# Projecting the last 512 tokens' values within attention instead of ahead of it

## The chip, the cores and the metric

The kernel runs on one core of a Trainium2 chip. The core has five engines that run their own instruction streams: TensorE (PE in the profile; its weight loads are shown apart as PEld), VectorE (DVE), ScalarE (ACT), GpSimd (POOL) and SyncE (SP, which here issues the DMAs). The metric is the device time of one execution in microseconds (us); lower is better. The kernel before takes 2252.64 us, the median of three runs (2252.49 to 2254.42).

## What is computed

One decoder block on 2048 tokens of 1024 channels. Cut to the part that matters here:

```python
h = rmsnorm(x, g_mix_pre) * (1.0 + scale_m) + shift_m
q, k, v, u = split(h @ w_in, [512, 1024, 1536])       # 512 channels each
attn = stick_breaking_attention(heads(q), heads(k), heads(v))   # 8 heads of 64 channels
pool = pooling_mixer(u, w_pool, pool_scale)
x = x + gate_m * rmsnorm(concat(attn, pool) @ w_out, g_mix_post)
# then a SwiGLU FFN of width 2816 in the same sandwich
```

Stick-breaking attention is causal: for each query, sigmoid(-z) of the earlier keys is multiplied up from the nearest key outwards, and a key's weight is sigmoid(z) times that product. Everything is float32. A float32 product is made of three TensorE matmuls on operands that are split in a high part (a cast to the `fp32r` type) and a low part (what is left): high x high, high x low, low x high.

## The kernel before

**Blocks.** The 2048 tokens are four blocks of 512 (`tb` 0 to 3). [...]

**Stages.** First the conditioning vectors and the q, k and u projections of blocks 0 and 1. Then the **v stage** (170 to 271 us in the profile): `v_pieces` projects the values of all 2048 tokens, block by block in the order 1, 0, 2, 3, each in four groups of 128 tokens (tokens as the stationary operand, all 512 value channels as the moving one; 8 pieces of 3 matmuls a group). Each group's result goes to `store_v`: ACT casts the high part into a tile `ve`, DVE subtracts for the low part, and SP stores it to `vd[tb]` in HBM. `weave` puts side work between the pieces: it is given generators with a first piece and a distance, and takes one step of a generator whenever the count of pieces has reached its next place. Among them are `token_ops(2)` and `token_ops(3)` (normalising and turning the tokens of blocks 2 and 3) and `out_weight_ops`, which loads w_out in 16 jobs of 128 x 512 floats, splits each in two (ACT the high part, POOL or DVE the low one, into `wo_parts`, which has four places), multiplies the first eight jobs by the pooling maps (three matmuls into a bank `wf`, then a split of that), and stores both parts in `wod`. One job loads 256 KB and stores 512 KB.

Then **attention** (from 271 us to about 790 us). Its work is a list of 320 steps (80 units of a head, a query block and a key block, four steps each). A step gives TensorE two score matmuls `z`, up to four transposes of a finished weight tile (`wt`, 128 x 128 each), and two value matmuls `av`. ACT takes two sigmoids of `z` and the cast of `wt`; DVE the running product (a scan along the keys) and the low part of `wt`; POOL the product of the two. In a diagonal unit (query block = key block) the four steps are 128, 256, 384 and 512 keys wide, in the others all are 512 wide: 32 diagonal units and 48 full ones.

**Filler.** Between the steps stand the projections of q, k and u for blocks 2 and 3, as **filler**: `pieces` makes them in tasks of 8 pieces of 3 matmuls (weights of 128 channels as the stationary operand, 512 tokens as the moving one), with one more empty piece per task. 12 chunks of 128 channels and two blocks make 24 tasks. The main loop takes as many pieces as the share of attention already done asks for (`goal`, spread over the first 79 of the 80 units), so a larger number of pieces is spread more densely over the same steps. The result of a task is taken out of its PSUM bank by `take_chunk`: a q or k chunk is split by ACT and DVE into a tile `e` of the pool `wst` (one buffer), and stored.

**Order.** For PE, ACT, DVE and POOL the order of instructions is the order of the program (`manual_schedule`). A step's place in the loop is thus its place in each engine's queue. The order of DMAs on SP is left to the scheduler. Memory of the v stage is used again by attention: the first `pr` tiles (the running products) lie where the last `ve` tiles lay, so they wait until those tiles' stores have landed.

In attention the transposes' results go to three PSUM banks in turn (`t_ps`: w0, w1, a1), the scores to two, and the filler to one (`mm`).

Of the kernel before, what the change touches and what calls it, by code (L numbers as in the profile page):

```python
# [9 lines left out]
F32 = mybir.dt.float32  # L10
# [34 lines left out]
def block_kernel(ctx, tc, x, c, w_cond, b_cond, g_mix_pre, g_mix_post, w_in, w_pool,  # L45
# [11 lines left out]
    def split(hi, lo, src, low=nc.vector):  # L57

        nc.scalar.copy(hi, src)  # L59
        low.tensor_tensor(lo, src, raw(hi), ALU.subtract)  # L60
# [285 lines left out]
    def token_ops(tb):  # L346

        new_tokens(tb)
        xs = normed_rows(tb, 0)
        yield  # L350
        for j in range(4):
            nxt = normed_rows(tb, j + 1) if j < 3 else None
            yield from put_tokens(tb, j, xs)
            xs = nxt
# [80 lines left out]
            else:  # L435
                op()

    base = {"q": 0, "k": SBW, "u": 3 * SBW}

    def chunk_load(chunk, th, pair=None, w32=None):  # L440
        kind, m = chunk
# [59 lines left out]
    def take_chunk(chunk, tb, ps):  # L501
        kind, m = chunk
        if kind == "u":
            ops = pool_ops(tb, ps, m)
            urgent.append(next(ops))
            small.append(ops)
        else:
            urgent.append(lambda: store_qk(tb, ps, (qd if kind == "q" else kd)[m], f"{kind}{m}"))

    def v_pieces(wvs, pool):  # L510
        for tb in (1, 0, 2, 3):
            for j in range(4):
                if (tb, j) == (1, 3):
                    turn[0] += 1
                ps = mm_ps(f"v{tb}_{j}")
                cols = slice(j * P, (j + 1) * P)
                for k in range(KC):
                    mm3(ps, [(tokens(tb, k, cols), (wvs[0][:, k, :], wvs[1][:, k, :]))],
                        first=k == 0, last=k == KC - 1)
                    if k == KC - 1:  # L520
                        urgent.append(lambda a=(tb, j, ps, pool): store_v(*a))
                    run_small()
                    yield
# [11 lines left out]
    def weave(main, sides):  # L535

        done = [0] * len(sides)
        for n, _ in enumerate(main):
            for i, (ops, first, every) in enumerate(sides):
                if n >= first + done[i] * every:  # L540
                    done[i] += 1
                    next(ops, None)
        for ops, _, _ in sides:
            for _ in ops:
                pass
# [265 lines left out]
    def pool_map_ops():  # L811

        pool = wvs[0]
        p32 = spare[:, 0].rearrange("p (k n) -> p k n", k=KC)
        nc.sync.dma_start(p32[:, 0:NG], w_pool.rearrange("g p n -> p g n"))
        yield
        for g in range(NG):
            wp.append([pool.tile([P, P], F32R, tag=f"wp{n}{g}", bufs=1, name=f"wp{n}{g}") for n in "hl"])
            pt = t_ps(f"wpt{g}")
            nc.tensor.transpose(pt[:, 0:P], p32[:, g], ident)  # L820
            nc.vector.tensor_scalar_mul(p32[:, g], pt[:, 0:P], colv[:, 64 + g:65 + g])
            yield
            split(*wp[g], p32[:, g])
            yield

    def out_weight_ops():

        w32 = hc.tile([P, KC, TB], F32, tag="hi", name="wo32")
        parts = hc.tile([P, 2, 4, TB], F32R, tag="lo", name="wo_parts")
        jobs = [(k, half) for k in (4, 5, 6, 7, 0, 1, 2, 3) for half in range(2)]  # L830

        def load(i):
            k, half = jobs[i]
            nc.sync.dma_start(w32[:, i % KC], w_out[k * P:(k + 1) * P, half * TB:(half + 1) * TB])

        def store(i):
            k, half = jobs[i]
            for l in range(2):
                nc.sync.dma_start(wod[k][l][:, half * TB:(half + 1) * TB], raw(parts[:, l, i % 4]))

        for i in range(4):
            load(i)
        for _ in range(6):
            yield
        pss = {}
        for i in range(len(jobs) + 1):
            if i < len(jobs):
                split(parts[:, 0, i % 4], parts[:, 1, i % 4], w32[:, i % KC], (nc.gpsimd, nc.vector)[i % 2])
                if jobs[i][0] < 4:
                    store(i)  # L850
            if i + 4 < len(jobs):
                load(i + 4)
            yield
            if i in pss:
                split(parts[:, 0, (i - 2) % 4], parts[:, 1, (i - 2) % 4], pss[i])
                store(i - 2)
                yield
            if i and jobs[i - 1][0] >= 4:
                pss[i + 1] = av_ps(f"wf{i}")
                mm3(pss[i + 1], [(wp[jobs[i - 1][0] - 4], (parts[:, 0, (i - 1) % 4], parts[:, 1, (i - 1) % 4]))])  # L860
                yield
# [4 lines left out]
    def first_filler_ops():  # L866
        for part in range(4):
            chunk_split(first_filler, part)
            yield
# [17 lines left out]
    def first_unit_loads():  # L887
        qts[0, 0] = wst.tile([P, 2, TB], F32R, tag="e", bufs=1, name="qt0_0")
        load_queries(qts[0, 0], 0, 0)
        yield  # L890
        load_keys(up.tile([P, TB], F32R, tag="um", bufs=2, name="kt0_0"),
                  up.tile([P, 16 + TB], F32R, tag="us0", name="vt0_0")[:, 0:TB].rearrange("p (b e) -> p b e", e=P), 0, 0)
        yield

    weave(v_pieces(wvs[1:], wvs[0]), [(token_ops(2), 30, 3), (token_ops(3), 62, 3), (pool_map_ops(), 2, 2), (out_weight_ops(), 34, 2), (first_filler_ops(), 20, 4), (first_unit_loads(), 108, 6)])
    drain_small()
    pro.close()

# [6 lines left out]
    def block_loads(h, tb):  # L905
        qt = qkp.tile([P, 2, TB], F32R, tag="qt", name=f"qt{h}_{tb}")
        load_queries(qt, h, tb)
        for sc in {0: (0,), 1: (1,), 2: (2, 1, 0), 3: (3,)}[tb]:
            load_keys(qkp.tile([P, TB], F32R, tag="kt", bufs=6, name=f"kt{h}_{tb}_{sc}"),
                      att.tile([P, 4, P], F32R, tag="vt", bufs=6, name=f"vt{h}_{tb}_{sc}"), h, sc)  # L910
        return qt
# [73 lines left out]
    def unit_loads(u):  # L985
        h, tb, sc = u
        if sc == tb and (h, tb) not in qts:
            assert tb < 2 or {("q", h // 2, tb), ("k", h // 2, tb)} <= stored
            qts[h, tb] = block_loads(h, tb)

    chunks = []
    for hp in range(4):
        chunks += [("q", hp), ("k", hp)]
        chunks += [("u", g) for g in {1: (0,), 3: (1, 2, 3)}.get(hp, ())]

    def fillers():
# [1 line left out]
        while urgent:  # L998
            urgent.pop(0)()

    tasks = [(n, tb) for n in range(len(chunks) - 2) for tb in (2, 3)]
    tasks += [(n, tb) for tb in (2, 3) for n in (len(chunks) - 2, len(chunks) - 1)]
    fill = fillers()
    N_PIECES = 9 * 2 * len(chunks) + 1
    units = [(h, tb, sc) for half in range(2) for h in range(HEADS) for tb in (2 * half, 2 * half + 1) for sc in range(tb, -1, -1)]
    area = [2.5 if tb == sc else 4.0 for _, tb, sc in units]
    wo, wo_next = [], 0
# [859 lines left out]
```

## Time and profile before

The profile is of one execution, whose span is 2250.0 us; the median of the runs, 2252.64 us, is 2.64 us above that span, which is what lies around it and the difference from run to run.

| stage, us from the span's start | what TensorE does | PE busy | DVE busy | ACT busy | POOL busy |
|---|---|---|---|---|---|
| 170 to 272 | values, side work | 102.00 of 102 | 48.32 | 53.32 | 28.64 |
| 272 to 815 | attention with filler, first products with w_out | 538.44 of 543 | 514.66 | 473.73 | 427.45 |
| 1100 to 1150 | FFN products alone, a piece of the stage that runs to the end | 50.00 of 50 | 33.39 | 14.14 | 40.02 |

How to read it: "busy" sums the time of an engine's instructions. A matmul is shown longer than the distance to the next one, since they are pipelined and their ends are modelled (389 ns are shown for a 128x512 matmul, though the next one starts 227 ns later). DVE and ACT instructions overlap their followers too, by some 0.1 us. So whether an engine still has room is read from the distance between starts in the timeline, not from its busy share.

### The profile page before, as it was taken

The numbers are of one execution on the slowest core, as the hardware profiler recorded it, in microseconds if no ns is written. First come the engines' busy times: TensorE is split into PE (matmuls) and PEld (weight loads), VectorE is DVE, ScalarE is ACT, GpSimd is POOL, SyncE is SP. The second block draws the span as 40 slices with busy tenths as digits, with TensorE's granted clock in tenths as the row PEclk, the third lists the DMA queues.
The fourth block names the chain that finished last, engine by engine and source line by source line (L and its number), as shares of the span: only waits on it lengthen the run. The fifth ranks groups of instructions, "written<-read, shape, count | busy, mean of one in ns | idle before, by whom it ended". The sixth has DMA issues, their size and how long they took to land.

```text
span 2250.0 us, 33310 instructions
## 1 busy us (share of the span) xinstructions
PE 2227.7 (99%) x10613; PEld 1844.9 (82%) x10613; DVE 1612.7 (72%) x2227; ACT 1168.1 (52%) x2425; POOL 1270.2 (56%) x1579
## 2 busy tenths in 40 slices
PE   8999999999999999999999999999999999999998
PEld 6888888888888888888888888888888888888887
DVE  7874599999999956666565656787965565655566
ACT  6335599898999944453232323555532323234444
POOL 1452277787779955546868687221677565651003
PEclk9999999999999999999999999999999999999999
DMA  9996877534443556665555556777853333328664
GB/s 317 343 283 212 282 205 183 148 107 114 121 123 104 164 178 221 226 203 170 162 161 159 164 162 209 252 233 244 253 169 122 94 117 94 116 90 297 213 188 149
DMA packets 324205, 413.56 MB, mean 184 GB/s; under 512 B 20855, under 2 KB 189371, under 8 KB 323901
## 3 DMA queue, kind: packets, MB, share of 16 engines
q1 hardware_dynamic: 319420, 408.81, 57.4%
q10 hardware_dynamic: 4608, 2.63, 0.4%
q8 instruction: 83, 1.36, 0.3%
q14 instruction: 94, 0.76, 0.1%
HBM read 282.90 MB, written 128.45 MB: 183 GB/s over the span
## 4 chain that ended last, share of the span: by engine, by line
PE 86%; DVE 5%; POOL 3%; issue 2%; ACT 2%; DMA 1%; DVEq 0%; POOLq 0%; ACTq 0%
PE wt L961 4%; PE t_g L71 4%; PE t_u L70 4%; PE t_g L70 4%; PE t_u L71 4%; PE t_u L69 4%; PE t_g L69 4%; PE dn0p L69 3%; PE dn0p L71 3%; PE dn0p L70 3%; PE dn1p L69 3%; PE dn1p L70 3%; PE dn1p L71 3%; PE b_u L70 3%; PE b_g L70 3%; PE b_g L71 3%
## 5 line engine op out<-in xcount | busy, mean ns | idle before, releaser
L950 POOL TENSOR_TENSOR w<-sg,pr 128x512 f32<-128x512 f32 (+2 forms) x320 | 306.3, 957 | 46.4 <-DVE pr L945 13.8
L1350 POOL TENSOR_TENSOR s<-s,cu 128x512 f32<-128x512 f32 x88 | 133.4, 1521 | 236.9 <-DVE cu L1349 128.3
L945 DVE TENSOR_TENSOR_SCAN pr<-pr,carry,begin 128x512 f32<-128x512 f32 x192 | 244.3, 1273 | 0.0
L929 ACT ACTIVATE sg<-z 128x512 f32<-128x512 f32 (+2 forms) x320 | 183.1, 572 | 50.9 <-PE z L927 40.5
L60 DVE TENSOR_TENSOR wtl<-wt,wth 128x512 fp32r<-128x512 f32 (+1 forms) x320 | 190.2, 594 | 17.8 <-ACT wth L59 15.5
L59 ACT CAST wth<-wt 128x512 fp32r<-128x512 f32 (+1 forms) x320 | 181.8, 568 | 10.4 <-PE wt L961 8.0
L931 ACT ACTIVATE pr<-z 128x512 f32<-128x512 f32 (+2 forms) x320 | 182.2, 569 | 0.0
L961 PE MATMUL wt<-ident,w 128*128 128x128 f32 x1088 | 172.3, 273 | 1.5 <-POOL pr L941 1.1
L60 DVE TENSOR_TENSOR u_s_l<-u_s,u_s_h 128x512 fp32r<-128x512 f32 x66 | 64.1, 971 | 151.2 <-ACT u_s_h L59 151.1
L961 PEld LDWEIGHTS wt<-ident,w 128*128 128x128 f32 x1088 | 134.1, 140 | 32.7 <-POOL pr L941 1.8
L1340 ACT ACTIVATE s<-s 128x512 f32<-128x512 f32 x88 | 55.7, 632 | 180.5 <-DVE s L1339 180.5
L976 PE MATMUL av<-wth,vt 128*128 128x512 f32 (+1 forms) x320 | 126.1, 394 | 0.9 <-ACT o L981 0.8
L60 DVE TENSOR_TENSOR u_a_l<-u,u_a_h 128x512 fp32r<-128x512 f32 x66 | 72.9, 1105 | 65.6 <-ACT u_a_h L59 65.4
L69 PE MATMUL dn0p<-w0p_h,g0p_h 128*128 128x512 f32 x308 | 119.8, 389 | 0.0
L70 PE MATMUL dn0p<-w0p_l,g0p_h 128*128 128x512 f32 x308 | 119.8, 389 | 0.0
L71 PE MATMUL dn0p<-w0p_h,g0p_l 128*128 128x512 f32 x308 | 119.8, 389 | 0.0
L926 PE MATMUL z<-kt,qt 128*128 128x512 f32 (+2 forms) x320 | 118.6, 371 | 0.7 <-ACT pr L931 0.6
L977 PE MATMUL av<-wtl,vt 128*128 128x512 f32 (+1 forms) x320 | 117.8, 368 | 1.3 <-DVE wtl L60 1.2
L59 ACT CAST u_s_h<-u_s 128x512 fp32r<-128x512 f32 x66 | 38.6, 614 | 151.9 <-POOL u_s L1282 150.2
L927 PE MATMUL z<-kt,qt 128*128 128x512 f32 (+2 forms) x320 | 117.0, 365 | 0.0
L59 ACT CAST g_s_h<-g_s 128x512 fp32r<-128x512 f32 x66 | 39.5, 621 | 148.2 <-POOL g_s L1282 72.0
L69 PE MATMUL dn1p<-w1p_h,g1p_h 128*128 128x512 f32 x292 | 113.6, 389 | 0.0
(657 smaller groups left out, 7173.1 us busy)
## 6 DMA issues: line engine op xcount, KB each, us to landing
g<-in_w_gate_dram SPq DMA_DIRECT2D x42, 512.0 KB, 5.4
u<-in_w_up_dram SPq DMA_DIRECT2D x42, 512.0 KB, 4.4
wc<-in_w_cond_dram SPq DMA_DIRECT2D x32, 512.0 KB, 7.6
qt<-qd SPq DMA_DIRECT2D x64, 256.0 KB, 4.0
kt<-kd SPq DMA_DIRECT2D x96, 128.0 KB, 3.6
vt<-vd SPq DMA_DIRECT2D x48, 256.0 KB, 3.9
wd<-in_w_down_dram SPq DMA_DIRECT2D x44, 256.0 KB, 3.7
tdt<-wd SPq DMA_DIRECT2D x44, 256.0 KB, 2.0
```

Of the source, the lines that this page charges most:

```text
L59: nc.scalar.copy(hi, src)
L60: low.tensor_tensor(lo, src, raw(hi), ALU.subtract)
L69: nc.tensor.matmul(ps, lh, rh, start=first and i == 0, stop=False)
L70: nc.tensor.matmul(ps, lh, rl, start=False, stop=False)
L71: nc.tensor.matmul(ps, ll, rh, start=False, stop=last and i == n - 1)
L929: nc.scalar.activation(sg[:, 0:L], z[:, 0:L], AF.Sigmoid, scale=0.125)
L931: nc.scalar.activation(pr[:, 0:L], z[:, 0:L], AF.Sigmoid, scale=-0.125)
L945: nc.vector.tensor_tensor_scan(keys, keys, begin, carry, ALU.mult, ALU.bypass)
L950: nc.gpsimd.tensor_tensor(w[:, 0:L], sg[:, 0:L], pr[:, 1:L + 1], ALU.mult)
L961: nc.tensor.transpose(wt[:, i * P:(i + 1) * P], wss[u][i][:, b * P:(b + 1) * P], ident)
L976: nc.tensor.matmul(av[:, lo0:], vb, wh[:, lo0:], start=first, stop=False)
L1350: nc.gpsimd.tensor_tensor(s, s, u, ALU.mult)
```

## The change

```diff
-    base = {"q": 0, "k": SBW, "u": 3 * SBW}
+    base = {"q": 0, "k": SBW, "v": 2 * SBW, "u": 3 * SBW}
...
             small.append(ops)
+        elif kind == "v":
+            urgent.extend(turn_values(tb, ps, m))
         else:
             urgent.append(lambda: store_qk(tb, ps, (qd if kind == "q" else kd)[m], f"{kind}{m}"))
 
+    def turn_values(tb, ps, hp):
+
+        v32 = att.tile([P, TB], F32, tag="v32", bufs=1, name=f"v32_{hp}")
+
+        def turn():
+            pt = t_ps(f"vt{hp}")
+            for j in range(4):
+                nc.tensor.transpose(pt[:, j * P:(j + 1) * P], v32[:, j * P:(j + 1) * P], ident)
+            ve = wst.tile([P, HEADS, 2, DH], F32R, tag="e", bufs=1, name=f"ve{tb}_{hp}")
+            split(ve[:, :, 0, :], ve[:, :, 1, :], pt.rearrange("p (g d) -> p g d", d=DH))
+            nc.sync.dma_start(vd[tb].rearrange("(j p) h e -> p j h e", p=P)[:, :, 2 * hp:2 * hp + 2, :],
+                              raw(ve.rearrange("p (j h) l d -> p j h (l d)", h=2)))
+            stored.add(("v", hp, tb))
+
+        return [lambda: nc.scalar.copy(v32, ps), lambda: None, turn]
+
     def v_pieces(wvs, pool):
-        for tb in (1, 0, 2, 3):
+        for tb in (1, 0, 2):
...
-    weave(v_pieces(wvs[1:], wvs[0]), [(token_ops(2), 30, 3), (token_ops(3), 62, 3), (pool_map_ops(), 2, 2), (out_weight_ops(), 34, 2), (first_filler_ops(), 20, 4), (first_unit_loads(), 108, 6)])
+    weave(v_pieces(wvs[1:], wvs[0]), [(token_ops(2), 30, 3), (token_ops(3), 62, 3), (pool_map_ops(), 2, 2), (out_weight_ops(), 34, 1.5), (first_filler_ops(), 20, 4), (first_unit_loads(), 82, 6)])
...
             assert tb < 2 or {("q", h // 2, tb), ("k", h // 2, tb)} <= stored
+            assert tb < 3 or ("v", h // 2, tb) in stored
...
-        chunks += [("q", hp), ("k", hp)]
+        chunks += [("q", hp), ("k", hp), ("v", hp)]
...
-    tasks = [(n, tb) for n in range(len(chunks) - 2) for tb in (2, 3)]
+    tasks = [(n, tb) for n in range(len(chunks) - 2) for tb in (2, 3) if chunks[n][0] != "v" or tb == 3]
...
-    N_PIECES = 9 * 2 * len(chunks) + 1
+    N_PIECES = 9 * len(tasks) + 1
```

The values of block 3 leave the v stage: 96 of its 384 matmuls go, with four `store_v`. They come back as four tasks of filler in attention, one for each pair of heads, placed behind that pair's q and k: 96 matmuls again, now with the value weights stationary, so that the result has channels on the partitions and tokens along the row. It must be turned: ACT copies the bank to `v32`, TensorE makes four transposes into a bank of `t_ps`, ACT and DVE split that into `ve`, and SP stores it. The chunk's weights (512 KB a chunk) are loaded and split as other chunks' are, in four parts by ACT and POOL. There are 28 tasks in place of 24, 253 pieces in place of 217. In the v stage, which now has 96 pieces in place of 128, a step of `out_weight_ops` is taken every 1.5 pieces in place of 2, and the loads of the first unit are asked for from piece 82 in place of 108.

The instruction orders below are those of the two programs, without times. A name's numbers count its buffers; lines of the changed kernel are 18 further on behind the new function, and 19 behind the changed list of tasks.

On ACT, at the end of the v stage, before (`wo_parts` is a half of a job's split, `ve` the cast of a group of values, `sg` and `pr` the first sigmoids of attention):

```order
L59 CAST wo_parts_1910<-wf8_2453 128x512
L59 CAST wo_parts_1910<-wo32_1909 128x512 x3
L59 CAST ve3_0_2518<-v3_0_2475 128x8x64
L59 CAST wo_parts_1910<-wo32_1909 128x512 x3
L59 CAST ve3_1_2562<-v3_1_2522 128x8x64
L59 CAST ve3_2_2596<-v3_2_2566 128x8x64
L59 CAST ve3_3_2625<-v3_3_2600 128x8x64
L929 ACTIVATE sg0_0_0_0_2665<-z0_0_0_0_2662 128x128
L931 ACTIVATE pr0_0_0_0_2667<-z0_0_0_0_2662 128x128
```

and now:

```order
L59 CAST ve2_2_2461<-v2_2_2379 128x8x64
L59 CAST wo_parts_1910<-wo32_1909 128x512 x2
L337 CAST hth3_2166<-x3_3_h1_2451 128x4x128
L59 CAST wo_parts_1910<-wo32_1909 128x512
L59 CAST ve2_3_2509<-v2_3_2469 128x8x64
L947 ACTIVATE sg0_0_0_0_2549<-z0_0_0_0_2546 128x128
L949 ACTIVATE pr0_0_0_0_2551<-z0_0_0_0_2546 128x128
```

Three casts of values stood between the last split of w_out and attention's first sigmoid; now one does.

On SP, the DMAs at the same place, before (`wod` are the stores of w_out, `vd` those of values, `qt`, `kt` and `vt` the loads of attention's second unit):

```order
L839 DMA wod3_173<-wo_parts_1910 128x512 x4
L528 DMA vd3_95<-ve3_1_2562 128x1024
L528 DMA vd3_95<-ve3_2_2596 128x1024
L876 DMA qt0_1_2721<-qd0_1_61 64x2x512 x2
L882 DMA kt0_1_1_2724<-kd0_1_77 64x512
L528 DMA vd3_95<-ve3_3_2625 128x1024
L882 DMA kt0_1_1_2724<-kd0_1_77 64x512
```

and now:

```order
L546 DMA vd2_94<-ve2_2_2461 128x1024
L857 DMA wod2_172<-wo_parts_1910 128x512
L857 DMA wod3_173<-wo_parts_1910 128x512 x4
L546 DMA vd2_94<-ve2_3_2509 128x1024
L894 DMA qt0_1_2605<-qd0_1_61 64x2x512 x2
L900 DMA kt0_1_1_2608<-kd0_1_77 64x512 x2
L901 DMA vt0_1_1_2609<-vd1_93 128x4x128
```

Between the last stores of w_out and the loads of the second unit there is one store of values now, in place of three.

On PE, in attention, where the first turned values now stand (`q1_2` is the filler's next task, `vt0_4032` the bank of turned values, `av` attention's own products with the loaded values `vt4_0_0`); before, no such rows exist:

```order
L69 MATMUL q1_2_4005<-hth2_1858,wq1_1_h_3659 128x512
L70 MATMUL q1_2_4005<-htl2_1859,wq1_1_h_3659 128x512
L71 MATMUL q1_2_4005<-hth2_1858,wq1_1_l_3660 128x512
L519 MATMUL vt0_4032<-ident_180,v32_0_3932 128x128 x4
L994 MATMUL av4_0_4026<-wth4_0_0_1_3977,vt4_0_0_3749 128x384
L995 MATMUL av4_0_4026<-wtl4_0_0_1_3978,vt4_0_0_3749 128x384
```

The four transposes stand behind a piece of the next task, two pieces after the copy to `v32` was put in ACT's queue.

## The prediction

> **What bounds the kernel now.** First the page's busy times, then the windows by stage (columns: PE, PEld, DVE, ACT and POOL busy with their counts, granted clock, DMA share, GB/s), since an average over the span says nothing of one stage.
>
> ```profile
> PE 2227.7 (99%) x10613; PEld 1844.9 (82%) x10613; DVE 1612.7 (72%) x2227; ACT 1168.1 (52%) x2425; POOL 1270.2 (56%) x1579
> 206.00:244.00 38.00, 38.00 (x190) 31.40 (x189) 26.56 (x55) 28.82 (x63) 15.03 (x15) 1.00 0.71 243
> 244.00:266.00 22.00, 22.00 (x98) 18.21 (x98) 8.29 (x11) 8.42 (x16) 6.63 (x5) 1.00 0.96 359
> 273.50:412.20 138.70, 135.90 (x793) 114.78 (x792) 132.28 (x190) 125.29 (x312) 98.08 (x230) 1.00 0.74 197
> 412.20:788.70 376.50, 374.74 (x2102) 312.50 (x2101) 367.40 (x458) 339.84 (x752) 315.31 (x675) 1.00 0.44 124
> 1100.00:1150.00 50.00, 50.00 (x222) 41.44 (x221) 33.39 (x40) 14.14 (x26) 40.02 (x27) 1.00 0.51 162
> ```
>
> In the v stage PE has no gap, at a full clock. In attention (the rows that start at 273.50 and 412.20, together 515.2 us) PE and DVE are both near their whole time, so busy shares can't tell which one leads. The distances between starts can. PE in mid-attention, most of a full step and then a piece of filler (start, length, engine, line):
>
> ```profile
> 551.91 0.39 PE L977 MATMUL av<-wtl,vt 128*128 128x512 f32 x1
> 552.14 0.39 PE L926 MATMUL z<-kt,qt 128*128 128x512 f32 x1
> 552.38 0.39 PE L927 MATMUL z<-kt,qt 128*128 128x512 f32 x1
> 552.61 0.60 PE L961 MATMUL wt<-ident,w 128*128 128x128 f32 x4
> 552.96 0.48 PE L69 MATMUL k<-hth,wk_h 128*128 128x512 f32 x1
> 553.28 0.40 PE L70 MATMUL k<-htl,wk_h 128*128 128x512 f32 x1
> 553.51 0.40 PE L71 MATMUL k<-hth,wk_l 128*128 128x512 f32 x1
> 553.75 0.39 PE L976 MATMUL av<-wth,vt 128*128 128x512 f32 x1
> ```
>
> A 128x512 matmul starts 0.233 us after the one before (551.91 to 552.61, three of them); four transposes take 0.35, and the matmul after the next one comes 0.08 late, so 0.11 a transpose. There is no gap: with its filler PE is full. All of attention by these prices: scores and values are 2 x 2 x (32 diagonal units x 2.5 + 48 x 4) = 1088 matmuls of 512 columns, the filler 24 x 24 less 9 ahead of it = 567, the transposes 1088: 1655 x 0.233 + 1088 x 0.11 = **505.3 of 515.2 us**. PE stands idle 9.9 us by this count, and 4.6 us by the busy times of the two windows. DVE by the same reading:
>
> ```profile
> 562.02 1.27 DVE L942 TENSOR_TENSOR_SCAN pr<-pr,zero,begin 128x512 f32<-128x512 f32 x1
> 563.21 0.67 DVE L60 TENSOR_TENSOR wtl<-wt,wth 128x512 fp32r<-128x512 f32 x1
> 563.79 0.68 DVE L60 TENSOR_TENSOR k<-k,k 128x512 fp32r<-128x512 f32 x1
> 564.39 1.27 DVE L945 TENSOR_TENSOR_SCAN pr<-pr,carry,begin 128x512 f32<-128x512 f32 x1
> ...
> L945 DVE TENSOR_TENSOR_SCAN pr<-pr,carry,begin 128x512 f32<-128x512 f32 x189 | 240.6, 1273 | 0.0
> L60 DVE TENSOR_TENSOR wtl<-wt,wth 128x512 fp32r<-128x512 f32 (+3 forms) x310 | 183.4, 592 | 12.2 <-ACT wth L59 10.0
> L942 DVE TENSOR_TENSOR_SCAN pr<-pr,zero,begin 128x128 f32<-128x128 f32 (+3 forms) x128 | 111.5, 873 | 1.7 <-ACT pr L931 1.7
> ```
>
> A full scan holds DVE 1.19 us, a full low part 0.58, that is 0.08 and 0.09 less than shown; the groups of attention (its records lack a few) then give 192 x 1.19 + 128 x 0.79 + 320 x 0.50 + 24 x 0.60 = **504 us**. PE and DVE are balanced at 98%; what is added to either is on the path, but for the few us in which it waits for the other.
>
> **The change, part by part.** *What leaves the v stage.* The four groups of block 3 run from the first of these rows to the second:
>
> ```profile
> 249.71 0.39 PE L69 MATMUL v<-wvh,hth 128*128 128x512 f32 x1
> ...
> 271.47 0.39 PE L69 MATMUL q<-hth,wq_h 128*128 128x512 f32 x1
> ```
>
> 96 matmuls, 21.8 us, PE alone on the path: **-21.8**. Their casts and low parts stood beside them and give nothing.
>
> *What comes into attention.* 96 matmuls x 0.233 = 22.4 and 16 transposes x 0.11 = 1.8: **+24.2** on PE. DVE gets four low parts, 4 x 0.60 = 2.4; it would then need 507 us where PE needs 529.5, so it no longer sets the pace.
>
> ```profile
> L981 ACT COPY o<-av 128x512 f32<-128x512 f32 x17 | 10.8, 635 | 0.0
> L454 ACT CAST wu_h<-wu 128x256 fp32r<-128x256 f32 x16 | 7.6, 473 | 0.0
> L458 POOL TENSOR_TENSOR wu_l<-wu,wu_h 128x256 fp32r<-128x256 f32 x16 | 11.8, 737 | 0.0
> ```
>
> ACT gets four copies and four casts at about 0.63 and 16 parts of weights at 0.47, 12.6 us; POOL 16 parts at 0.74, 11.8 us, on 413 busy of 515. Both are hidden behind PE, and four loads and stores of 512 KB behind a DMA share of 0.44 to 0.74; were POOL's cover gone near the end of attention, one chunk's parts cost 3 us. Each turn takes one of the three banks that the `wt` rows need next: 0 to 0.5 us, four times; I take 0, as all of PE's gaps in the two windows, these banks' among them, are 4.6 us.
>
> *What PE's idle time takes up.* Denser filler fills gaps in which PE now waits for DVE. All of the 9.9 us is the upper bound, nothing the lower (gaps from other causes, such as the start). With DVE down from 98% to 95% I take two thirds: **-6.5**.
>
> *w_out's splits.* A wf product follows its split by the same number of steps, now 1.5 pieces each in place of 2. Two such jobs:
>
> ```profile
> 227.33 1.29 POOL L338 TENSOR_TENSOR htl<-x_h,hth 128x512 fp32r<-128x512 f32 x1 [3.39 <-ACT hth L337]
> 227.80 1.37 DVE L60 TENSOR_TENSOR wo_parts<-wo,wo_parts 128x512 fp32r<-128x512 f32 x1 [1.20 <-ACT wo_parts L59]
> 230.67 0.48 PE L69 MATMUL wf<-wo_parts,wph 128*128 128x512 f32 x1
> ...
> 233.16 0.61 ACT L59 CAST wo_parts<-wo 128x512 fp32r<-128x512 f32 x1
> 234.58 1.30 POOL L60 TENSOR_TENSOR wo_parts<-wo,wo_parts 128x512 fp32r<-128x512 f32 x1
> 236.39 0.48 PE L69 MATMUL wf<-wo_parts,wph 128*128 128x512 f32 x1
> ```
>
> The split ends 1.5 and 0.5 us ahead of its product. A quarter less distance takes at least 1.0 us away (three steps, 0.5 pieces each, a piece being 3 x 0.227 us); the first then still holds, the second is 0.5 late, and PE, whose queue is in order, waits with the next value group behind it. For eight jobs 0 to 3 us; I take **+1**.
>
> ```profile
> L60 DVE TENSOR_TENSOR wo_parts<-wo,wo_parts 128x512 fp32r<-128x512 f32 x8 | 7.2, 895 | 6.1 <-ACT wo_parts L59 5.0 <-DMA wod<-wo_parts 1.1
> L60 DVE TENSOR_TENSOR wo_parts<-wf,wo_parts 128x512 fp32r<-128x512 f32 x8 | 5.5, 684 | 2.4 <-ACT wo_parts L59 2.4
> ```
>
> The same subtraction on DVE takes 0.21 us more with both inputs in SBUF than with one in PSUM. [...]
>
> *The start of attention.* Now it comes 1.5 us behind the last group of block 2, with w_out's stores still going out:
>
> ```profile
> 259.81 2.60 SPq L839 DMA_DIRECT2D wod<-wo_parts  x4
> 262.51 5.38 SPq L528 DMA_DIRECT2D vd<-ve  x2
> 267.94 1.27 SPq L876 DMA_DIRECT2D qt<-qd  x2
> ...
> 276.31 0.49 ACT L931 ACTIVATE pr<-z 128x384 f32<-128x384 f32 x1
> ...
> vd<-ve SPq DMA_DIRECT2D x7, 512.0 KB, 3.4
> ...
> POOL pr L941 <- DMA vd<-ve: 11.7, 1, 11.7
> ```
>
> Before, the stores of w_out were issued by 262.4, 9 us ahead of 271.47. From 206 to 266 the DMAs moved 243 GB/s x 38 us + 359 x 22 = 17.1 MB; without the two stores of block 3's values among it 16.1 MB, which at 359 GB/s take 45 us, so the last bytes land at 251 at the earliest, against PE's start at 249.7; with the pauses of the early part, 254 to 258. The last `ve` store stands behind w_out's and takes 3.4 us at best: issued at 251.5, landed at 255. The third `pr` needs it; before it came 4.8 us behind PE's start, so it would be wanted at 254.5. Late by 0.5 us at best and some 5 at worst; I take **+2**. What waits: ACT and POOL at `pr`, behind them the scans, and with two score banks PE within two steps.
>
> Sum: -21.8 + 24.2 - 6.5 + 1 + 2 = **-1.1**. The execution's span of 2250.0 becomes 2248.9, and with the 2.64 us by which the median of the runs stands above it **2251.5**.
>
> **The rivals.** *All idle time taken up, nothing late.* If PE's gaps are only DVE's doing and the DMAs keep pace: -21.8 + 24.2 - 9.9 = -7.5, **2245**. For it: DVE's share falls by 3 points everywhere. Against: gaps remain at the start and where POOL lags.
>
> *PE has room that its start distances hide.* If the share in which PE loads no weights (88 of 515 us in the two windows) were free, the filler would cost only DVE's 2.4: -21.8 + 2.4 + 3, **2236**. [...] Against: in 1100 to 1150 the loads take the same 83%, while 222 matmuls stand in 50 us with no gap, so this share is what a full PE shows here.
>
> *Slower: the stores of w_out hold up attention.* SP's queue is in order, and `parts` has four places. If a split must wait for a store, the splits do not come sooner, whatever the table says, and ACT, with attention's sigmoids behind them, starts late: 5 us there, 3 at the wf products, and a start without scans leaves more idle, 2 taken up: -21.8 + 24.2 - 2 + 8 = +8.4, **2261**. It decides if the last store of w_out is issued later than about 252. For it: a DMA share of 0.96 already. Against: 0.71 before that leaves room.
>
> **How the numbers follow.** A run can tell about 0.2%, 4.5 us, from no change. Forecast 0.54 (2251.5, its own range 2248 to 2257); all taken up 0.24; free room 0.03; slower 0.19. So faster 0.27, same 0.54, slower 0.19. The range takes in nearly all of the first rival and the nearer half of the slower one, 2245 to 2259; the bounds of all terms together would reach from 2245 to 2265.
>
> **What would show it.** Attention's first `z` at 252 to 253 and its last step some 17 to 19 us later after it than the 515 us of now; no PE gap behind filler; DVE's idle time in attention up by some 15 us; PE waiting for `wo_parts` in the v stage, and `pr` for `vd` at its end. Wrong would be an attention that grows by well under 14 us (PE had room) or starts after 256 (the DMAs decide).

## The result, and the profile after

The changed kernel takes **2260.39 us** (median of 6 runs, 2258.79 to 2263.38), the kernel before beside it 2252.90 (6 runs, 2251.95 to 2254.42): a ratio of 1.0034, 95% interval 1.0023 to 1.0046. The change makes the kernel 7.5 us slower.

The profiled execution took 2262.16 us, its span is 2260.3. First the page's line of busy times, then the windows by stage (columns as in the prediction), cut where the stages start and end in this trace: the v stage; from its last matmul to attention's first `z`; head 0 up to the second unit's first `z`; the rest of head 0; the other heads of the first half; the second half.

```profile
PE 2231.2 (99%) x10629; PEld 1851.9 (82%) x10629; DVE 1619.3 (72%) x2227; ACT 1176.6 (52%) x2445; POOL 1279.0 (57%) x1595
172.22:252.82 80.60, 79.10 (x381) 64.88 (x379) 42.29 (x89) 47.34 (x103) 25.51 (x26) 1.00 0.75 249
252.82:257.07 4.25, 2.59 (x12) 1.80 (x11) 2.77 (x3) 3.83 (x8) 2.97 (x3) 1.00 0.87 327
257.07:267.24 10.17, 5.17 (x24) 3.77 (x23) 5.63 (x10) 3.65 (x9) 2.18 (x7) 0.97 1.05 316
267.24:280.06 12.82, 12.82 (x55) 10.80 (x56) 8.62 (x12) 9.29 (x24) 7.90 (x19) 0.76 0.65 160
280.06:407.93 127.87, 126.11 (x748) 108.28 (x746) 120.52 (x175) 115.22 (x288) 91.16 (x210) 1.00 0.76 198
407.93:799.04 391.11, 389.86 (x2183) 327.16 (x2181) 372.67 (x461) 348.06 (x769) 323.31 (x687) 1.00 0.44 127
```

The same stretches of the kernel before:

```profile
170.64:271.24 100.60, 100.60 (x476) 82.91 (x475) 48.32 (x97) 52.99 (x113) 28.64 (x29) 1.00 0.72 252
271.24:273.51 2.27, 2.27 (x11) 1.88 (x10) 1.11 (x2) 0.59 (x1) 0.00 (x0) 1.00 0.59 124
273.51:278.26 4.75, 4.75 (x25) 4.00 (x23) 2.60 (x5) 2.48 (x8) 1.40 (x5) 1.00 1.03 275
278.26:289.51 11.25, 9.94 (x52) 7.84 (x51) 9.77 (x13) 10.09 (x26) 8.30 (x21) 1.00 0.79 212
289.51:412.17 122.66, 121.17 (x720) 102.91 (x719) 119.87 (x173) 112.69 (x281) 88.39 (x206) 1.00 0.72 193
412.17:788.69 376.52, 374.76 (x2102) 312.52 (x2100) 367.42 (x458) 339.86 (x752) 315.30 (x675) 1.00 0.44 124
```

Row by row, after less before: -20.0, +2.0, +5.4, +1.6, +5.2, +14.6, together +8.8; behind the last `z` nothing differs (1461.3 us in both). The two spans differ by 10.3; the other 1.6 us lies ahead of the v stage (172.22 against 170.64). There this execution shows a halved clock twice, in stretches of 3.41 us that begin at 24 and 48 us (granted clock 0.83 in each of these windows of 10 us):

```profile
20.00:30.00 10.00, 9.61 (x45) 7.26 (x44) 7.75 (x19) 7.90 (x16) 0.97 (x2) 0.83 1.10 356
45.00:55.00 10.00, 10.00 (x51) 8.41 (x51) 8.46 (x18) 5.54 (x8) 0.00 (x0) 0.83 0.50 149
```

Some executions show these two stretches and others don't, and a variant of the kernel before (`e13_before_no_late_stores` below) shows them too (a granted clock of 0.83 in both windows); so they are not the change's. What the change did: the v stage gives back nearly all that was expected, attention's body (rows five and six) takes 19.8 more, and **the start of attention, rows two to four, costs 9.0**. TensorE's waits from 170 to 275 us of the changed kernel, of which the same list of the kernel before has none up to its first `z` (engine, what it was to start, what released it; sum, count, longest):

```profile
PE z L944 <- DMA kt<-kd: 4.7, 1, 4.7
PE q L69 <- DVE ve L60: 1.7, 1, 1.7
PE wf L70 <- POOL wo_parts L60: 1.5, 1, 1.5
PE z L944 <- DVE ve L60: 0.3, 1, 0.3
```

The last stores and the first loads on SP's queue, then ACT and PE, from the timeline of the changed kernel (start, length; in brackets the idle time before and what ended it):

```profile
246.16 8.79 SPq L857 DMA_DIRECT2D wod<-wo_parts  x10
255.04 0.38 SPq L546 DMA_DIRECT2D vd<-ve  x1
255.52 3.47 SPq L857 DMA_DIRECT2D wod<-wo_parts  x5
259.08 0.60 SPq L546 DMA_DIRECT2D vd<-ve  x1
259.73 1.91 SPq L894 DMA_DIRECT2D qt<-qd  x2
261.68 1.27 SPq L900 DMA_DIRECT2D kt<-kd  x2
...
250.55 1.14 ACT L59 CAST wo_parts<-wo 128x512 fp32r<-128x512 f32 x2 [4.82 <-DMA wod<-wo_parts]
253.48 0.60 ACT L59 CAST ve<-v 128x512 fp32r<-128x512 f32 x1
263.88 0.49 ACT L949 ACTIVATE pr<-z 128x384 f32<-128x384 f32 x1 [2.64 <-DMA vd<-ve]
...
267.24 0.45 PE L944 MATMUL z<-kt,qt 128*128 128x128 f32 x1 [4.68 <-DMA kt<-kd]
268.23 0.63 PE L69 MATMUL q<-hth,wq_h 128*128 128x512 f32 x1
268.66 0.63 PE L70 MATMUL q<-htl,wq_h 128*128 128x512 f32 x1
```

SP issues w_out's stores, with one store of values between them, to 259.0, 2 us *behind* the first `z` (257.07); in the kernel before the last went out at 262.4, 11 us ahead of its first `z` (273.51). The second unit's `qt` and `kt` stand behind them. ACT waited 4.8 us for a store to free a place of `wo_parts`, with the cast of values behind it in its queue; that makes TensorE's wait of 1.7 us for `ve`. And after 4.7 us of idleness a 128x512 matmul starts every 0.43 us (268.23 to 268.66), where it was 0.23: the clock is halved from 266.6 on, for 6.83 us (granted clock 0.50 from 266.56 to 273.39, 1.00 before and after).

### The profile page after: what moved, and what is told of

The parts are those of the page before. It is cut to its first block, busy times and chain, and to the rows that moved or that the text cites. A ratio compares the mean times of both kernels' runs of the same rounds, so it can differ in the third digit from the quotient of the medians.

```text
span 2260.3 us, 33374 instructions
## 1 busy us (share of the span) xinstructions
PE 2231.2 (99%) x10629; PEld 1851.9 (82%) x10629; DVE 1619.3 (72%) x2227; ACT 1176.6 (52%) x2445; POOL 1279.0 (57%) x1595
## 4 chain that ended last, share of the span: by engine, by line
PE 90%; POOL 2%; DVE 2%; issue 2%; DMA 1%; ACT 1%; SPq 0%; DVEq 0%; POOLq 0%; ACTq 0%
PE wt L979 5%; PE t_g L71 4%; PE t_g L69 4%; PE t_u L69 4%; PE t_u L71 4%; PE t_g L70 4%; PE t_u L70 4%; PE dn0p L70 3%; PE dn0p L71 3%; PE dn0p L69 3%; PE z L944 3%; PE av L995 3%; PE av L994 3%; PE z L945 3%; PE dn1p L70 3%; PE dn1p L71 3%
## 5 line engine op out<-in xcount | busy, mean ns | idle before, releaser
L60 DVE TENSOR_TENSOR wtl<-wt,wth 128x512 fp32r<-128x512 f32 (+1 forms) x320 | 190.6, 596 | 33.2 <-ACT wth L59 30.0
L60 DVE TENSOR_TENSOR u_s_l<-u_s,u_s_h 128x512 fp32r<-128x512 f32 x66 | 65.2, 988 | 150.0 <-ACT u_s_h L59 149.9
L60 DVE TENSOR_TENSOR u_a_l<-u,u_a_h 128x512 fp32r<-128x512 f32 x66 | 73.5, 1115 | 66.0 <-ACT u_a_h L59 66.0
L69 PE MATMUL dn0p<-w0p_h,g0p_h 128*128 128x512 f32 x308 | 120.0, 390 | 0.0
L960 DVE TENSOR_TENSOR_SCAN pr<-pr,zero,begin 128x128 f32<-128x128 f32 (+3 forms) x128 | 111.4, 871 | 6.4 <-ACT pr L949 6.3
```

What stands on the lines that cost most here:

```text
L69: nc.tensor.matmul(ps, lh, rh, start=first and i == 0, stop=False)
```

## The experiments

Two theories stood at first. *Stores*: w_out's stores, squeezed against the end of a shorter v stage, hold up attention's first loads. *Attention*: the added filler costs more there than counted. A third, *spacing*, blames the closer distance itself. Medians are against 2260.39 (the changed kernel, measured once, with 6 runs) and 2252.5 to 2253.1 (the kernel before, measured beside each group of runs); so a difference from the changed kernel can be some 0.6 us off for the chip alone. Each kernel ran 5 or 11 times.

### The closer spacing alone: 2256.64

```diff
# the kernel before
-(out_weight_ops(), 34, 2)
+(out_weight_ops(), 34, 1.5)
```

> The kernel before, with one part of the change alone: w_out's operations follow each other every 1.5 pieces in place of 2. Theories for the 7.5 us that the change cost: (stores) the stores of w_out, squeezed against the end of a shorter v stage, fill the DMAs and hold up the first loads of attention; (attention) the added filler and its turns cost more within attention than they save; (spacing) the closer spacing itself costs, because the wf products wait for GpSimd's splits. Stores: here the v stage keeps its 128 pieces, so the last stores are issued some 20 us earlier than attention begins, and the time is that of the kernel before or a little less, 2250 to 2253.5. Attention: the same, 2252 to 2253.5. Spacing: 2254.5 to 2258, with TensorE waiting in row wf <- POOL wo_parts for 1.5 us or more.

Ratio 1.0018 (1.0009 to 1.0027), +3.9 us. *Stores* is wrong here and *spacing* hit its range, though for more than its own reason. TensorE waits 1.5 us at `wf`, as expected, and 2.3 us for evicted values, and the latter comes from a store:

```profile
250.43 1.14 ACT L59 CAST wo_parts<-wo 128x512 fp32r<-128x512 f32 x2 [5.22 <-DMA wod<-wo_parts]
253.36 0.60 ACT L59 CAST ve<-v 128x512 fp32r<-128x512 f32 x1
254.74 0.50 PE L69 MATMUL v<-wvh,hth 128*128 128x512 f32 x1 [2.32 <-DVE ve L60]
```

Closer steps do not make the stores faster; they make ACT's queue run into them, even in a stage of full length.

### What the filler costs in attention: 2239.79 without it

```diff
-        chunks += [("q", hp), ("k", hp), ("v", hp)]
+        chunks += [("q", hp), ("k", hp)]
...
-        nc.sync.dma_start(raw(vt), vd[sc][:, h, :].rearrange("(b p) e -> p b e", p=P))
+        nc.sync.dma_start(raw(vt), vd[min(sc, 2)][:, h, :].rearrange("(b p) e -> p b e", p=P))
```

> The changed kernel without the filler of the last 512 tokens' values: their 96 products and 16 turns are left out altogether, and attention reads the values of the 512 tokens ahead of them in their place. The difference from the changed kernel is what the filler costs within attention. By the growth of attention after its first head in the two traces it is 19.8 us: 2239.5 to 2242. By the prediction's terms, 24.2 less 6.5, it is 17.7: 2242 to 2244. By count alone, with no idle time taken up, 24.2: 2236. Stores: the wait at the start of attention stays as it is, since nothing ahead of it changes. Attention as the cause of the loss: the wait would go with the filler and the difference come to 27 us or more, 2234 or less.

20.6 us less by the medians. By the traces attention takes 522.2 us from first to last `z`, 19.8 less than the changed kernel, and the wait for `kt` is there with 4.4 us. *Attention* falls as the cause of the loss: the body costs what the two traces had shown, and the start is late without the filler too.

### Turns done twice: 2262.74

```diff
-            for j in range(4):
+            for j in range(8):
+                j %= 4
                 nc.tensor.transpose(pt[:, j * P:(j + 1) * P], v32[:, j * P:(j + 1) * P], ident)
```

> The changed kernel, with each of the four values' turns done twice into the same bank, 16 transposes more in attention. If turns stand on TensorE's path, 16 x 0.11 us make it 1.8 us slower than the changed kernel's 2260.4: 2261.5 to 2263.5. If TensorE has idle time that hides them, 2259.5 to 2261. If holding a turning bank longer is what costs (attention's own turns behind it), over 2264.

2.3 us more. In the second half of attention, where 12 of the 16 stand, 392.48 us in place of 391.11: 0.11 us each, on the path, and no sign that the longer use of a bank costs anything.

### Half of the late stores, and all of them: 2255.40 and 2255.83

```diff
# half: the low parts of rows 0 to 511
-            for l in range(2):
+            for l in range(2 if k >= 4 else 1):
                 nc.sync.dma_start(wod[k][l][:, half * TB:(half + 1) * TB], raw(parts[:, l, i % 4]))
# all: both parts
-                if jobs[i][0] < 4:
-                    store(i)
```

> The changed kernel, with the eight stores of the low parts of w_out's rows 0 to 511 left out; the loads after attention read the high parts in their place, so it leaves out those low parts of the sum. Every split and every product stays. 8 x 256 KB are 2.1 MB, 6 us at the 340 GB/s that the DMAs moved in that stretch. Stores: the wait for kt shrinks by about 5 us or goes, and the half clock with it; 2250 to 2255. Attention and spacing: no change, 2259 to 2262.

> The changed kernel, with all sixteen stores of w_out's rows 0 to 511 left out (the splits stay, and the loads after attention read the stored products in their place, so these rows' part of the sum is another). Stores: with half of them gone the time fell by 5.0 us; now the rest of the waits that begin with them goes too (1.7 us for the evicted values, 4.7 us for kt, 3.4 us of halved clock; the 1.5 us wait of wf stays), so 2249 to 2252.5, first z at 252 to 254.5, clock 1.00 throughout attention. If the wait for kt has another source (the values' own store, the length of the queue): 2254 to 2256, no better than with half of the stores.

Half of them out: 5.0 us less, though 0.4 above the range of *stores*, and the wait for `kt` does not go: it is still 3.2 us. The first `z` comes 1.6 us sooner after the start of the v stage, and the granted clock is 0.83 from 260 to 270 and 1.00 from 270 to 300, which is a halved clock for some 3.4 us in place of 6.83. All of them out: no better, and *stores* alone misses its range. In its profile (the fastest of eleven runs that spread from 2253.5 to 2259.8) 2.6 us of the wait stay, and SP's own waits say why:

```profile
SPq L892 <- DVE wo_parts L60: 2.7, 1, 2.7
```

And DVE in the timeline:

```profile
254.84 0.68 DVE L60 TENSOR_TENSOR wo_parts<-wo,wo_parts 128x512 fp32r<-128x512 f32 x1
```

The second unit's `qt` (L892 here) now waits for the last *split* of w_out, which ends at 255.5. The same stores left out of the kernel before, as the control:

> The kernel before, with the same sixteen stores left out, as the control. TensorE waits for nothing there between 140 and 270 us, so under every theory 2251.5 to 2253.5. If it falls by more than 1.5 us, the stores cost something in the kernel before too, and the gain of the same edit in the changed kernel isn't the change's alone.

2253.33, ratio 1.0004 (0.9995 to 1.0012): there they cost nothing.

### Is it the turning of x? 2261.43, and 2257.09 without the late stores

```diff
-(token_ops(3), 62, 3)
+(token_ops(3), 62, 2)
```

> The changed kernel, with the operations that turn x's last 512 rows (token_ops(3)) every 2 pieces of the v stage in place of 3, so that they end at piece 80 in place of 89. Without any late store TensorE still waited 2.6 us for kt. A second theory for the start of attention (tokens): in the kernel before, the turning of x ended at 247.6, 24 us ahead of the v stage's end, and the second unit's loads were issued at 267.9, 5.6 us ahead of the first z; in the changed kernel the turning ends at 257.2, since the stage under it is 32 pieces shorter, and the second unit's loads, whose buffers lie where the turning's lay, come at 259.7, 2.7 us behind the first z. Tokens alone: the loads come 5 us or more earlier, and the time falls to 2251 to 2255. Stores alone: the loads are held by the stores as they are, 2259 to 2262. Both, one behind the other: the stores still end last, 2257 to 2261, and the gain shows only with the stores out of the way.

> The same, with the sixteen stores of w_out's rows 0 to 511 left out as well (those rows' part of the sum is another). Without the stores alone the time was 2255.8. Tokens, or both one behind the other: the wait for kt goes, first z stays at 252.5 to 255, 2250 to 2253.5. If the buffers aren't freed by the turning but by something else at the end of the stage (the last evicted values): no change, 2254.5 to 2257.

The turning ends at 248.2, 9 us sooner, and `qt` is issued at 261.5, no sooner at all. Without the late stores it is issued at 255.5, as in `e12_no_late_stores` (255.6). The theory falls in both kernels, as far as they can tell: with the turning closer TensorE also waits 3.0 and 2.8 us for `x_h`, the turned x, which it did not before.

### The whole tail of w_out out: 2253.65

```diff
-        jobs = [(k, half) for k in (4, 5, 6, 7, 0, 1, 2, 3) for half in range(2)]
+        jobs = [(k, half) for k in (4, 5, 6, 7) for half in range(2)]
```

(Lines beside it let the loop finish its last product. In all kernels that leave out stores the loads behind attention read other stored parts in their place.)

> The changed kernel without the last eight of w_out's jobs altogether (loads, splits and stores of rows 0 to 511; attention's successor reads the stored products in their place, so those rows' part of the sum is another). With only their stores left out, the second unit's load of q waited for the last of these splits (2.7 us, DVE wo_parts), and 2.6 us of the wait for kt stayed. Tail of w_out (splits and stores alike, since they end at the end of a stage that is 32 pieces shorter): the loads of the second unit are issued ahead of the first z, as in the kernel before, the wait for kt goes, 2250 to 2253, with 1.5 us of the wait of wf left. If the second unit's loads wait for the last values' eviction: no better than 2255.

> The kernel before, without the same eight jobs, as the control: its last split ends 14 us and its last store is issued 11 us ahead of the first z, and TensorE waits for neither, so 2251 to 2253.5 under every theory.

6.7 us less, ratio to the kernel before 1.0000 (0.9991 to 1.0008); the control is at 2253.26, 1.0002 (0.9993 to 1.0011). SP's queue in the timeline of this kernel:

```profile
243.43 2.24 SPq L857 DMA_DIRECT2D wod<-wo_parts  x2
245.76 1.29 SPq L894 DMA_DIRECT2D qt<-qd  x2
249.18 0.33 SPq L546 DMA_DIRECT2D vd<-ve  x1
249.56 1.25 SPq L900 DMA_DIRECT2D kt<-kd  x2
```

Its windows of head 0:

```profile
253.93:258.68 4.75, 4.75 (x25) 4.00 (x24) 2.33 (x5) 2.47 (x8) 1.13 (x4) 1.00 0.99 265
258.68:270.06 11.38, 10.37 (x55) 8.47 (x54) 9.52 (x14) 10.08 (x27) 8.27 (x20) 1.00 0.75 213
```

With the tail gone `kt` is issued 4.4 us ahead of the first `z`, and head 0 takes 4.75 + 11.38 us, as in the kernel before (4.75 + 11.25). This settles the start of attention: **the last jobs of w_out, their splits and their stores**, hold the second unit's loads. This execution, the slowest of the eleven, loses 2.9 us later, in attention's body: `av` waits 3.1 us for ACT's copy of a finished output (`o`), whose one buffer is still being stored, and behind it the clock is halved for some 3.4 us (granted clock 0.66 from 385 to 390, 1.00 before and after). In the changed kernel the same wait has 1.7 us, with no such stretch, in the kernel before 0.4 at most.

### The idle time, or the clock behind it? 2257.36

```diff
                 unit_loads(u)
+            if n == 4:
+                pt = t_ps("keep")
+                for j in range(40):
+                    nc.tensor.transpose(pt[:, j % 4 * P:(j % 4 + 1) * P], ident, ident)
             weights_step(u, i)
```

> The changed kernel, with 40 transposes that nobody reads put ahead of the first products of attention's second unit, where TensorE waits 4.7 us for kt; at some 0.11 us each they fill 4.4 us of it. Nothing comes earlier by them. If the idle time is what halves the granted clock for 6.8 us behind it, the clock stays at 1.00 and the time falls by about half of that, 3.4 us, to 2256 to 2258. If the clock falls for another reason, the dip stays and the time is 2260 to 2262. Attention as the cause (not the wait): 2260 to 2264.

The timeline of PE, then the windows of head 0:

```profile
262.24 4.53 PE L1122 MATMUL keep<-ident 128*128 128x128 f32 x40
266.57 0.30 PE L944 MATMUL z<-kt,qt 128*128 128x128 f32 x1
```

```profile
256.87:266.57 9.70, 9.36 (x64) 8.19 (x63) 5.74 (x10) 3.65 (x9) 2.19 (x7) 1.00 1.06 319
266.57:276.53 9.96, 9.96 (x57) 8.42 (x56) 8.02 (x12) 9.13 (x24) 7.43 (x18) 1.00 1.12 264
```

3.0 us less by work that nobody reads: `kt` comes hardly sooner (266.57 against 267.24), the clock stays at 1.00, and head 0 takes 19.7 us where it took 23.0, of which 2.9 are gained behind the wait (9.96 against 12.82). So here it is the idle time that halves the clock, and of the tail's 6.7 us about 3 are the clock.

### Ways out that weren't: 2254.22 at best

Work brought forward to fill the wait, w_out begun sooner, its two kinds of jobs in turn, and two paces:

```diff
# e4: seven pieces of filler ahead of the second unit
-        goal = min(START, START // 2 + n) + ...
+        goal = min(START, START // 2 + n) + (n > 2) * 7 * (1 - n / len(steps)) + ...
# e2
-(out_weight_ops(), 34, 1.5)
+(out_weight_ops(), 22, 1.5)
# e9
-        jobs = [(k, half) for k in (4, 5, 6, 7, 0, 1, 2, 3) for half in range(2)]
+        jobs = [(k, half) for m in range(HK) for half in range(2) for k in (HK + m, m)]
# e10: 22, 1.5 as e2, and (g2: 22, 1.4; f3: e10 with the turning of x closer)
                 if jobs[i][0] < 4:
                     store(i)
+                    yield
```

> The changed kernel, with up to seven pieces of the filler (21 products, some 4.9 us) brought forward to just ahead of attention's second unit, where TensorE waits 4.7 us for kt; the sum of the filler is the same, so later steps have less. Stores: the wait is filled with work that has to be done anyway, and the clock isn't halved behind it: 4.7 and 3.4 us less, 2251.5 to 2255. If the filler's own operands are late too (the next chunk's weights come by the same queue): 2256 to 2260. Attention: no gain, 2259 to 2262.

2264.48. The wait only changes its cause: the filler's own bank is not yet emptied (`PE q L69 <- DVE q L60`, 3.5 us), and attention takes 545.4 us from first to last `z`, 3.4 more than in the changed kernel, though its filler is the same. A miss; where the rest goes wasn't followed up.

> The changed kernel, with w_out's operations begun at piece 22 of the v stage in place of 34, still 1.5 pieces apart, so that they end 12 pieces (some 8 us) earlier. Stores: the loads of attention's second unit are no longer queued behind the w_out stores; TensorE's wait for kt of 4.7 us and the half clock behind it go, and the time falls by 6 to 11 us, to 2249 to 2254. Attention: the time stays within 1.5 us of the changed kernel's 2260.4. Spacing: it stays too, or rises, since the wf products keep their distance from the splits.

2266.89. A miss, and it shows the other side: the stores now stand in front of x's loads on SP's queue (ACT waits for `xt`, 8.5 us at the longest), and TensorE for the turned x, in its list of waits:

```profile
PE x_pt L132 <- DVE x_h L140: 11.8, 3, 7.4
```

> The changed kernel, with w_out's splits taken in another order: rows that go through a product and rows that don't take turns, in place of the first eight jobs of the one kind and then eight of the other, whose stores follow each other fastest. Start and distance of the operations, their number and their bytes stay. Stores (their crowding at the end): the DMAs move the same bytes evenly, the splits no longer wait for stores behind the evictions of the values, and kt comes in time; 2249 to 2254. If the sum of bytes ahead of attention is what counts and not their crowding: 2258 to 2262. Spacing: the wait of wf for GpSimd's split, 1.5 us, stays or becomes more.

2265.77. Inconclusive about crowding: in this order each product stands three steps behind its split in place of five, and all of the products' splits fall to GpSimd, so `wf` waits eight times, 10.3 us together. The wait for `kt` does shrink, to 1.3 us.

> The changed kernel, with w_out's operations begun at piece 22 and, behind each job that stores a split at once (rows 0 to 511), one step left empty: the first eight jobs come 8 us earlier, the last eight follow each other every 3 pieces in place of 1.5 and end at piece 92, as now. Beginning at 22 without the empty steps was 6.5 us slower than the changed kernel, as the loads of x queued behind the stores and TensorE waited 11.8 us for x_h. Stores: at half the pace neither x nor kt waits, 2250 to 2255. If the sum of bytes ahead of attention is what counts, the waits for x_h come back: 2258 to 2266.

2254.22, ratio 1.0009 (1.0000 to 1.0017): the best of the complete kernels with this change, 6.2 us under it, still not below the kernel before. TensorE waits 3.0 us for `x_h` and 1.5 us for `kt`.

> The whole computation, with w_out's operations begun at piece 22, the empty step behind each of the last eight jobs, and 1.4 pieces in place of 1.5 between operations, so that they end at piece 87 in place of 92 (2254.2 with 1.5, with waits of 3.0 us for x_h and 1.5 us for kt). Tail of w_out: the wait for kt goes; if x_h waits no longer than it did, 2251.5 to 2254. If x's loads are held longer by the same bytes in less time: 2255 to 2260, with more than 4 us of waits for x_h.

2256.02. No wait for `kt` any more, but 2.9 us for `x_h` and 1.4 us at `wf`. With x's turning closer (`f3_tokens_closer_two_paces`) it is 2256.53, with 4.1 us for `x_h` and 1.4 for `kt`, where 2250 to 2253 was expected if neither waited and 2255 to 2260 if x waited longer. No pace was found at which neither waits.

## Why the prediction was wrong

It said 2251.5, within 0.2% at 0.54, and 2245 to 2259; the time is 1.4 us above that range. By its own steps:

| step | predicted | measured | from |
|---|---|---|---|
| 96 matmuls leave the v stage | -21.8 | -21.8 | -20.0 of the row, less 1.5 at `wf` and 0.3 |
| `wf` products late | +1 (0 to 3) | +1.5 | one wait, the same in `e1_before_closer`; 0.3 more of row one has no wait to it |
| filler in attention, 24.2 less 6.5 | +17.7 | +19.8 | rows five and six; `e7_no_last_values` |
| turning banks | 0 | 0 | `e6_turn_twice` |
| start of attention | +2 (0.5 to 5) | +9.0 | rows two to four |

**The step that failed is the start of attention: "Late by 0.5 us at best and some 5 at worst; I take +2".** Its DMA estimate was near, and somewhat low: it put the last bytes at 254 to 258, and SP went on issuing stores to 259.0. What it priced was the wrong waiter. It looked at the third `pr`, which waits for the last `ve` store; that wait came (ACT, 2.6 us, until 263.88) but was not what held TensorE, which stood idle until 267.24. What TensorE waited for was `kt`, the load of the *second* unit. The order printed ahead of the prediction has it: `qt` and `kt` stand behind the last store of w_out on SP, and one store of values, in place of three, lies between. `g1_no_late_jobs` shows that nothing else held it. And the step put nothing for what idleness does to the clock, about 3 us in `e5_keep_busy`.

**The slower rival had the place and nearly the number**, 2261, with a chance of 0.19, but not the path: it too had ACT's sigmoids late, and not the load of `kt`; that the numbers meet is in part luck. Its deciding point, a last store later than about 252, was passed by 7 us. Against it stood only a DMA share of 0.71, taken over 206 to 244 us; but much of the DMAs' room lay ahead of that (shares of 0.27 and 0.55 at 170 to 180 and 180 to 190), where the splits had not begun (the first is at 206), and `e2_early` shows what using it costs. Its terms, 5 lost at the start, 3 at `wf` and 2 taken up, came out as 9, 1.5 and 4.4.

**The `wf` term** lay inside its bounds, but on a wrong count: in steady state a product stands five steps behind its split, not three, so the distance falls by 1.7 us, and by the prediction's own rows both jobs would have been late, by 0.2 and 1.2 us. One wait of 1.5 us came.

**The idle time taken up** was 4.4 us by the count (24.2 less 19.8), not 6.5, and inside the bounds given. The busy columns hardly show it: in rows five and six TensorE's idle time goes from 3.25 to 3.01 us, so most of the 4.4 would lie in gaps that the modelled ends of matmuls hide. This part of the account is argued, not shown. DVE's idle time in attention rose by 19 us (541.97 less 507.44 busy, against 515.18 less 499.66), not 15. By the count some 5 us of gaps are left there; the longest is the 1.7 us at `av` (ACT waits 2.4 us for the store of `o`), and the rest wasn't tried. The rival of free room behind the matmuls (2236) is wrong: the filler costs 19.8 of the 24.2 us of its start distances.

Even with nothing late the change would be worth 21.8 - 19.8 = 2.0 us, less than the bound of 0.2%. The signs named in advance were read rightly by the last of them: attention starts at 257.07, after 256, and "the DMAs decide".

## What to carry to other kernels

Work taken out of a stage takes away the cover of everything that ran under it: before counting the gain, list what must be finished at that stage's end (here 16 jobs of loads, splits and stores) and find, on the queue that issues them, the first thing that the next stage will wait for behind them. Setting such side work closer together in the program did not make the stores faster here; it moved waits into ACT (5.2 us for a store in `e1_before_closer`) and TensorE (2.3 us behind that). And a wait of TensorE of a few us can have a second price in the clock behind it: here 4.7 us of waiting, and about 3 us more by `e5_keep_busy`.

## What was not expected of the hardware

From the v stage on, these traces show the granted clock at a half for a few us behind gaps of TensorE. The wait for `kt` of 4.7 us (the changed kernel) was followed by 6.83 us of it, one of 3.2 (`e3_half_stores`) by some 3.4, one of 4.4 by 3.4 in `e6_turn_twice` and by 6.8 in `e7_no_last_values` (0.83 in one and in two windows of 10 us); one of 2.6 (`e12_no_late_stores`, 1.00 from 250 to 300) by none. In the changed kernel the stretches last 3.41, 3.41 and 6.83 us and begin at 24.22, 48.11 and 266.56: the distances of 23.89 and 218.45 us are 7 and 64 times 3.413 us. What sets these lengths and places was not shown. In `f2_tokens_closer_no_late_stores` two short gaps, of 0.84 and 0.70 us, were followed by a slower stretch as well. Its timeline of PE:

```profile
262.78 0.30 PE L942 MATMUL z<-kt,qt 128*128 128x128 f32 x1 [0.84 <-DMA kt<-kd]
264.23 0.50 PE L69 MATMUL q<-hth,wq_h 128*128 128x512 f32 x1 [0.70 <-DVE q L60]
265.52 0.63 PE L69 MATMUL q<-hth,wq_h 128*128 128x512 f32 x1
265.95 0.63 PE L70 MATMUL q<-htl,wq_h 128*128 128x512 f32 x1
```

From 265.52 to 267.23 the 128x512 matmuls start 0.43 us apart, where the distance ahead of that is 0.23 (264.57 to 264.80), though from 261.8 to 265.2, in 3.4 us, TensorE had started eight matmuls. So TensorE had not stood idle for all of that time, and two waits that are short by themselves cost more than their length here: by the author's estimate up to 1.7 us on top, if the stretch lasts 3.41 us as the short ones of the changed kernel do. Why the 2.6 us of `e12_no_late_stores` had no such stretch behind them, and how much idle time it takes, these runs don't say.

The two stretches at 24 and 48 us are another matter: in the 3.41 us ahead of them TensorE was busy for 3.18 and 3.41, though most of these matmuls had a single column (128x1). Whether that is why, and why only some executions show them, wasn't tried.
